# The down product in PSUM banks taken by name, in blocks of 512 columns, and six banks in turn for the products around the mixers

## The chip, the cores and the metric

The kernel runs on one core of one Trainium2 chip. The time is what the device takes from start to end of one launch, in microseconds; the value before is the median of three runs, 2753.59 us (2749.94, 2753.59, 2753.59). Beside them one execution was recorded by the hardware profiler; every duration below comes from that recording.

## The reference, cut to what matters

A decoder layer is computed for a prompt of 2048 tokens and for 8 sample sequences of 8 tokens (64 in all), with 1024 features. The part after the two mixers (a gated delta rule and a windowed attention) is:

```
x = x + g1 * (mix @ w_out)                          # out-projection, residual
h = rmsnorm(x) * (1 + sc2) + sh2
u = h @ ffn_w_up                                    # 1024 -> 2 x 2816
gate, up = split(causal_dwconv(u) + b)              # 3 taps
x = x + g2 * ((silu(gate) * up) @ ffn_w_down)       # 2816 -> 1024
y = rmsnorm(x, final_norm_w)
```

All values are float32.

## The kernel before

Features lie on the 128 partitions and tokens along the free axis, so a product is a weight tile of 128 x 128 that is loaded into TensorE and a block of tokens that streams past it. Every float32 operand is split into a high and a low part of a shorter type (a cast on ScalarE, L314 and L1600; the difference on VectorE, L315 and L1601), and each tile product is three matmuls: high by high, high by low, low by high. PSUM has eight banks of 512 float32 columns per partition, and a product accumulates in one bank until a vector engine reads it.

The stages follow each other: input projection and first mixers (to about 750 us), then `between(0)`, which does the out-projection of the first half (`outproj`, L1130 on, tile `op_ps`) and starts the up products (`up_proj`, L1209 on; the matmuls are those of `gemm_steps`, L323, tile `up_ps`). The other up groups of the first half fill TensorE beside the second set of mixers. `between(1)` does the same for the second half and starts the first six up groups of it. The rest of the second half's up products are done as `up_quarters`, by a Strassen scheme with few waits (L1503 and L323, tiles `uq_a`, `uq_u`, `uq_b`, `uq_g`, `uq_c`; ScalarE copies the last ones out in L1527). Each up result goes through a convolution (`conv`, L1427 on: taps on VectorE in a PSUM tile of three banks, `cq`, L1433) and the product of gate and up, `actq` (L1481), and lands in DRAM as `act_d`.

`outproj` and the ordinary up groups take their accumulator from two banks in turn (`acc_bank`, L394, and in `project`, L366, the tag "acc"): the matmul that starts a group waits until the group two earlier has been read. The readers are for `op_ps` the residual (VectorE, L1184; for the 64 sample columns L1187 and L1188) and for `up_ps` the taps (VectorE, L522) and copies with bias (ScalarE, L517).

`down_phase` (L1566 on) computes the last product with a Strassen-Winograd scheme: seven half-size products instead of eight. Its table `DOWN` names for each product the weight sum (A11, S2 and so on), the operand sum (B11, T2 and so on), the column group g, whether a fresh accumulator begins, and which output quarters the accumulator is added to. There are two passes of 512 columns each per half; in pass 2 the quarters of group 1 carry the 64 samples too, 576 columns. A product has KH = 11 k-steps; a k-step has four row tiles m, times two column blocks s (256 and 256, or 256 and 320), times three matmuls (L1690). So a product keeps eight accumulators, one in each bank.

Around the products: `get_w` and `get_t` load and split the operands, some k-steps ahead (DR = 6 ready, AHEAD = 3). Most operand sums were prepared in DRAM; T2 is made here from two loads and one VectorE subtraction (L1621), T4 from two loads and one addition (L1626). After the last k-steps of a product, taken bank by bank, `out` adds the accumulator to the output quarter (`residual`) and, from the fourth product on, adds its squares to a running sum (L1195, L1196). `norm` (L1646 on) turns these sums into a factor for each token by small matmuls (`ss_ps` in L214, `rb_ps` in L222, which also take a bank) and multiplies (L1654, L1660, L1662) and stores the output. It is a generator that is stepped between k-steps of the next product.

The eight banks came from a pool of their own, `psd`, with one tag and eight buffers, made after the quarters' pool was closed; which bank is which follows from the order of the requests. Where fewer than eight could be free (at the start, and where a norm was under way), the first LEAD = 5 k-steps ran on the first banks only ("head") and then on the others. These lines are in the part `if len(acc) < KT or not q` of `down_phase`.

The order of instructions on each engine is set by a scheduler from the program; each engine works through its own list in order, and a tile that is written again waits for its readers.

Of the kernel before, what the change touches and what calls it, by code (L numbers as in the profile page):

```python
# [14 lines left out]
F32 = mybir.dt.float32  # L15
# [7 lines left out]
P = 128  # L23
# [71 lines left out]
def kernel(  # L95
# [298 lines left out]
    def acc_bank(name):  # L394
        return pm.tile([P, 512], F32, tag="acc", name=name, bufs=BANKS["acc"])

# [732 lines left out]
    def outproj(hf, bis, mix, sums, op, kept=None):  # L1129
# [78 lines left out]

    def up_proj(hf, h, uc, op, ms=range(MU)):  # L1209
# [24 lines left out]
        return project(ms, "up_ps", lambda m: load_split(I["w_upT"][m]), h, hf, evac, turn=(3, 2), third=third)  # L1234
# [304 lines left out]
    def weight_sums(units, pool):  # L1539
# [3 lines left out]
        for i in units:  # L1543
# [22 lines left out]
    def down_phase(ds, dr, psd):  # L1566

        G, fw = MOD[:, 5], nw[:, 2]
        bk = lambda name: psd.tile([P, 512], F32, tag="dn", name=name)
# [61 lines left out]
        blocks_of = lambda q, g: [slice(0, SW), slice(SW, wide(q, g))]  # L1631
        queue = [(q, i, slice(0, wide(q, DOWN[q % ND][2]))) for q in range(Q - 1) for i in range(KH)]
        queue += [(Q - 1, i, blocks_of(Q - 1, 1)[s]) for s in (1, 0) for i in range(KH)]
# [12 lines left out]
        def norm(g, parts, x, sums, cols, last=False):  # L1646

            for off, n in parts:
# [6 lines left out]
                yield from token_rstd([a[:, off:off + n] for a in sums], n, rB, dr, bk)  # L1655
# [13 lines left out]
        for q in range(Q):  # L1669
# [6 lines left out]
            subs = blocks_of(q, g)  # L1676
            order = [(m, s) for m in range(NM) for s in range(2)]
            if new:
                banks = [bk("dn_ps") for _ in order] if not finish else [bk("dn_ps") for _ in order[:FREE]]

                acc = dict(zip(order, banks if q else banks[:1] + banks[4:] + banks[1:4]))
# [12 lines left out]
            def out(m, s):  # L1694
                for og, tg in outs:
# [3 lines left out]
                    residual(v, acc[m, s], n, min(n, SW), G[:, NM * og + m], v, dr)  # L1699
# [3 lines left out]
                    if first and s == 0:  # L1703
                        sums[tg] = [dr.tile([P, big], F32, tag=f"dsum{tg}", name=f"dsum{tg}", bufs=2)]
# [8 lines left out]
            lead = 0  # L1713
            if len(acc) < KT or not q:
                lead = LEAD
                head = order[:FREE if q else 5]
                for i in range(lead):
                    ahead(f + min(i + AHEAD, DR - 1))
                    products(i, head)
                    if finish and i in (1, 3):  # L1720
# [356 lines left out]
```

## Time and profile before

| | |
|---|---|
| median of three runs | 2753.59 us |
| profiled execution, its own time | 2747.36 us |
| its span | 2745.6 us |
| mean granted clock of TensorE | 0.985 |
| TensorE busy | 2638.5 us (96%) |
| VectorE, ScalarE, GpSimd busy | 69%, 47%, 29% |
| up quarters | 1815 to 2235 us |
| down | 2235 to 2745.6 us |

The profiled execution is 6.2 us faster than the median of the runs and lies 1.8 us outside its own span. PE is TensorE's matmul queue, PEld its weight loads, DVE VectorE, ACT ScalarE, POOL GpSimd, SP the queue that issues DMAs. A matmul's duration in the profile contains the filling of the array and overlaps with the next one: what a matmul costs is the distance between two starts.

### The profile page before, as it was taken

Reading aid. Unit: us, or ns where it says so; the run is one execution under the profiler, and the core shown is the slowest. Engines: PE = TensorE matmul, PEld = TensorE weight load, DVE = VectorE, ACT = ScalarE, POOL = GpSimd, SP = SyncE. Lnnn points to the kernel's source line nnn. Section 1 sums busy time; section 2 is a strip of 40 time slices with the busy share of each in tenths; the row PEclk is TensorE's granted clock in tenths of the full one; section 3 lists DMA queues with packets and bytes.
Section 4 is the critical chain, followed back from the end, with each engine's and each line's share of the span. In section 5 each row is a group of like instructions: output and inputs, shape, how many; then the busy total and the mean of one; then the engine's idle time right before and its main releaser. Section 6 shows DMA issues by size and latency. Waiting matters only on the chain.

```text
span 2745.6 us, 52204 instructions
## 1 busy us (share of the span) xinstructions
PE 2638.5 (96%) x19404; PEld 2472.7 (90%) x19404; DVE 1891.1 (69%) x3936; ACT 1300.8 (47%) x3394; POOL 807.1 (29%) x711
## 2 busy tenths in 40 slices
PE   7998999999999899999999999899999989999997
PEld 6898987788999898888888899899999989999997
DVE  7667479898403888888667654786777666677666
ACT  6444265554322654555444543554555544444443
POOL 2025143442313422222121204345655500022021
PEclk9999999999999999999999999999999999999998
DMA  7677443332345452332255335314555458567754
GB/s 281 232 267 242 117 139 104 91 100 77 129 114 192 130 146 78 99 92 74 85 177 177 133 122 183 113 66 162 166 174 193 158 184 282 184 222 266 237 179 155
DMA packets 319099, 433.99 MB, mean 158 GB/s; under 512 B 83155, under 2 KB 224436, under 8 KB 318580
## 3 DMA queue, kind: packets, MB, share of 16 engines
q1 hardware_dynamic: 318844, 430.66, 48.6%
q8 instruction: 152, 2.49, 0.4%
q14 instruction: 103, 0.84, 0.1%
HBM read 316.25 MB, written 115.33 MB: 157 GB/s over the span
## 4 chain that ended last, share of the span: by engine, by line
PE 64%; DVE 19%; DMA 8%; issue 4%; ACT 3%; POOL 2%; SPq 0%; DVEq 0%; ACTq 0%; POOLq 0%
PE up_ps L323 16%; PE in_ps L323 12%; PE dn_ps L1690 10%; PE op_ps L323 6%; PE uq_b L1503 4%; DVE ev L522 3%; PE uq_c L1503 2%; PE uq_g L1503 2%; PE uq_u L1503 1%; DVE ht L258 1%; PE pv_ps L954 1%; PE as_ps L917 1%; DMA tr<-T_d 1%; DVE gt L699 1%; DMA tx<-act_d 1%
## 5 line engine op out<-in xcount | busy, mean ns | idle before, releaser
L323 PE MATMUL up_ps<-hi,w_hi 128*128 128x384 f32 (+2 forms) x1152 | 378.1, 328 | 7.8 <-ACT cv L517 7.7
L323 PE MATMUL up_ps<-hi,w_lo 128*128 128x384 f32 (+2 forms) x1152 | 373.1, 324 | 3.7 <-DVE w_lo L315 3.7
L323 PE MATMUL up_ps<-lo,w_hi 128*128 128x384 f32 (+2 forms) x1152 | 370.5, 322 | 0.0
L323 PE MATMUL in_ps<-hi,w_hi 128*128 128x384 f32 (+2 forms) x1056 | 346.9, 333 | 5.1 <-DVE ev L572 1.8
L323 PE MATMUL in_ps<-lo,w_hi 128*128 128x384 f32 (+2 forms) x1056 | 349.2, 331 | 2.2 <-DVE lo L265 1.3
L323 PE MATMUL in_ps<-hi,w_lo 128*128 128x384 f32 (+2 forms) x1056 | 347.2, 329 | 1.2 <-POOL w_lo L315 1.2
L1690 PE MATMUL dn_ps<-th,wh 128*128 128x256 f32 (+1 forms) x1192 | 333.2, 289 | 13.7 <-DVE actq L1481 9.7
L1690 PE MATMUL dn_ps<-tl,wh 128*128 128x256 f32 (+1 forms) x1192 | 340.6, 289 | 2.8 <-DVE tl L1601 2.8
L1690 PE MATMUL dn_ps<-th,wl 128*128 128x256 f32 (+1 forms) x1192 | 338.7, 288 | 0.0
L323 PEld LDWEIGHTS up_ps<-hi,w_hi 128*128 128x128 f32 x1152 | 218.0, 189 | 28.3 <-issue 15.1
L1690 PEld LDWEIGHTS dn_ps<-th,wh 128*128 128x128 f32 x1192 | 225.8, 193 | 15.0 <-issue 9.9
L1690 PEld LDWEIGHTS dn_ps<-tl,wh 128*128 128x128 f32 x1192 | 229.6, 193 | 4.2 <-DVE tl L1601 4.1
L323 PEld LDWEIGHTS up_ps<-hi,w_lo 128*128 128x128 f32 x1152 | 217.8, 189 | 12.8 <-issue 7.0
L1690 PEld LDWEIGHTS dn_ps<-th,wl 128*128 128x128 f32 x1192 | 229.0, 193 | 0.0
L323 PEld LDWEIGHTS up_ps<-lo,w_hi 128*128 128x128 f32 x1152 | 218.0, 189 | 7.2 <-issue 6.2
L323 PEld LDWEIGHTS in_ps<-hi,w_hi 128*128 128x128 f32 x1056 | 200.3, 191 | 17.8 <-issue 9.7
L323 PEld LDWEIGHTS in_ps<-lo,w_hi 128*128 128x128 f32 x1056 | 202.0, 191 | 15.1 <-issue 9.5
L323 PEld LDWEIGHTS in_ps<-hi,w_lo 128*128 128x128 f32 x1056 | 201.9, 191 | 6.6 <-issue 4.4
L314 ACT CAST w_hi<-w_raw 128x1024 fp32r<-128x1024 f32 x124 | 129.7, 1047 | 117.4 <-PE op_ps L323 44.9
L315 DVE TENSOR_TENSOR w_lo<-w_raw,w_hi 128x1024 fp32r<-128x1024 f32 x95 | 118.1, 1243 | 93.2 <-ACT w_hi L314 91.7
L522 DVE SCALAR_TENSOR_TENSOR ev<-rb,cw,ev 128x384 f32<-128x384 f32 (+1 forms) x216 | 149.0, 696 | 38.0 <-ACT ev L515 35.9
L1601 DVE TENSOR_TENSOR wl<-wr,wh 128x512 fp32r<-128x512 f32 x149 | 107.4, 722 | 81.2 <-ACT wh L1600 79.2
(531 smaller groups left out, 6690.0 us busy)
## 6 DMA issues: line engine op xcount, KB each, us to landing
w_raw<-in_w_upT_dram SPq DMA_DIRECT2D x50, 512.0 KB
wada<-in_w_ada_dram SPq DMA_DIRECT2D x44, 512.0 KB
w_raw<-in_w_inT_dram SPq DMA_DIRECT2D x44, 512.0 KB
wr<-ws_d SPq DMA_DIRECT2D x88, 256.0 KB
proj<-ev SPq DMA_DIRECT2D x88, 192.0 KB
d<-act_d SPq DMA_DIRECT2D x33, 512.0 KB
wr<-in_w_downT_dram SPq DMA_DIRECT2D x66, 256.0 KB
tr<-T_d SPq DMA_DIRECT2D x66, 256.0 KB
```

The lines of the kernel that those rows point to most:

```text
L258: nc.vector.scalar_tensor_tensor(t, x, S[:, k, 0:1], rB[:, :np_], ALU.mult, ALU.mult)
L314: nc.scalar.copy(hi, raw)
L315: (eng or nc.vector).tensor_tensor(lo, raw, hi.bitcast(F32), ALU.subtract)
L323: nc.tensor.matmul(ps[:, :n], a[:, k, :], b[:, k, :n], start=first is not False and k == ks[0] and i == 0, stop=last is not False and k == ...
L522: nc.vector.scalar_tensor_tensor(out, src(j), w[:, j:j + 1], out, ALU.mult, ALU.add)
L699: nc.vector.tensor_tensor(tv, G[:np_, j, j + 1:].unsqueeze(2).broadcast_to(shape), T0[:, j, 0:j + 1].unsqueeze(1).broadcast_to(shape), ALU ...
L917: nc.tensor.matmul(banks[v][:, 256 * g + P * k0:256 * g + 256], qs[r, g0 + g], kw[r, P * k0:], start=True, stop=True, tile_position=(64 * ...
L954: nc.tensor.matmul(pv_ps[64 * v:64 * v + 64, :], (vprev[0], vt)[half][:, 64 * v:64 * v + 64], PT[v, half], start=half == k0, stop=half == 1)
L1503: nc.tensor.matmul(bk[t][:, :nb], u[:, k], v[:, k], start=new and k == 0 and y == 0, stop=k == KG - 1 and y == 2, skip_group_check=True)
L1601: nc.vector.tensor_tensor(l, raw, h.bitcast(F32), ALU.subtract)
L1690: nc.tensor.matmul(acc[m, s][:, :n], w[q, i][a][:, c], th[b][:, v], start=new and i == 0 and y == 0, stop=i == KH - 1 and y == 2, skip_gro ...
```

## The change

It has four parts.

- `down_phase` is handed the pool of the quarters, `pq`, and takes five of its banks by their names (a, u, b, g, c) and the three-bank tile `cq`, of which it uses each third as a bank. A list, `free`, rotates: a new set of accumulators takes the first entries, which then go to its end. The head-first k-steps are gone.
- A product that has no sample columns runs in one block of 512 columns, with four accumulators: all of pass 1, and in pass 2 the fourth and fifth product (S1 and S4, of group 2).
- In `DOWN` the product A22 with T4 is now the sixth and A12 with B21 the last. The norm that belongs to the end of pass 1 is stepped during the fourth product of pass 2 (it ran from its first), that of the fifth product of pass 2 during the last. The last product takes its blocks with the 320-column half first in the list of banks too.
- `free_bank` gives six banks in turn, two each of the tags "acc", "fr" and "at", to `op_ps`, and to `up_ps` in those groups that are begun in `between(0)` and from `between(1)` on.

```diff
+    FREE_TAGS = ("acc", "acc", "fr", "fr", "at", "at")
+    turns = [0]
+
+    def free_bank(name):
+        turns[0] += 1
+        return bank(name, FREE_TAGS[turns[0] % len(FREE_TAGS)])
...
-                ps = acc_bank("op_ps")
+                ps = free_bank("op_ps")
...
-        return project(ms, "up_ps", lambda m: load_split(I["w_upT"][m]), h, hf, evac, turn=(3, 2), third=third)
+        return project(ms, "up_ps", lambda m: load_split(I["w_upT"][m]), h, hf, evac, turn=(3, 2), third=third,
+                       tags=up_tags)
...
-            ("S1", "T1", 2, True, [(1, 2)]), ("S4", "B22", 2, False, [(0, 2)]), ("A12", "B21", 1, True, [(0, 1)]),
-            ("A22", "T4", 1, True, [(1, 1)])]
+            ("S1", "T1", 2, True, [(1, 2)]), ("S4", "B22", 2, False, [(0, 2)]), ("A22", "T4", 1, True, [(1, 1)]),
+            ("A12", "B21", 1, True, [(0, 1)])]
...
-        bk = lambda name: psd.tile([P, 512], F32, tag="dn", name=name)
+        free = [pq.tile([P, 512], F32, tag=t, name="dn_ps", bufs=1) for t in "aubgc"]
+
+        three = pq.tile([P, 3 * 512], F32, tag="cq", name="dn_ps", bufs=1)
+        free += [three[:, 512 * i:512 * i + 512] for i in range(3)]
...
-        blocks_of = lambda q, g: [slice(0, SW), slice(SW, wide(q, g))]
+        def blocks_of(q, g=None):
+
+            if q < ND or q % ND in (3, 4):
+                return [slice(0, PW)]
+            return [slice(0, SW), slice(SW, wide(q, g or DOWN[q % ND][2]))]
...
+            if last:
+                order = [(m, b) for b in (1, 0) for m in range(NM)]
             if new:
...
+                acc = dict(zip(order, free))
+                free = free[len(order):] + free[:len(order)]
...
-            if j == 4:
-                finish = norm(2, [(0, PW)], x, sums[2], cols[2])
+
+            if j == 4 and not ip:
+                finish = norm(2, [(0, PW)], x, sums[2], cols[2], free[4:6])
+            elif j == 4:
+                late = (2, [(0, PW)], x, sums[2], cols[2])
+            elif j == 5 and ip:
+                finish = norm(*late, free[-2:])
             elif j == 6:
-                finish = norm(1, [(0, PW)], x, sums[1], cols[1])
+                late = (1, [(0, PW)], x, sums[1], cols[1])
+            elif j == 2 and ip:
+                finish = norm(*late, free[-2:])
...
+            up_tags[:] = FREE_TAGS
             filler, _ = between(0, in_end(), es, range(MU))
+            up_tags[:] = ["acc"]
...
-        down_phase(ds, dr, new_pool(es, "psd", bufs=8, space=PSUM))
+        down_phase(ds, dr, pq)
```

Counted over the program, TensorE has 1188 matmuls fewer, VectorE 49 instructions fewer, ScalarE 24, GpSimd 21 and the DMA queue 11.

How the order of TensorE reads where the quarters end and down begins. Before (dn_ps_24944, 24948 and so on are single banks of the pool; behind a row, in brackets, the engines whose work it waits for):

```order
L323 MATMUL uq_b_24882<-hi2_19793,rl_21099 128x320
L1690 MATMUL dn_ps_24944<-th_24960,wh_24954 128x256 [waits Activation_49]
L1690 MATMUL dn_ps_24944<-tl_24961,wh_24954 128x256 [waits DVE_49]
L1690 MATMUL dn_ps_24944<-th_24960,wl_24955 128x256
L1690 MATMUL dn_ps_24948<-th_24960,wh_24954 128x256 [waits DVE_49,PE_49,Activation_49]
L1690 MATMUL dn_ps_24948<-tl_24961,wh_24954 128x256
L1690 MATMUL dn_ps_24948<-th_24960,wl_24955 128x256
L1690 MATMUL dn_ps_24949<-th_24960,wh_24954 128x256
```

Changed (dn_ps_24940 is bank a, 24941 u, 24942 b, 24943 g):

```order
L323 MATMUL uq_b_24882<-hi2_19793,rl_21099 128x320
L1713 MATMUL dn_ps_24940<-th_24954,wh_24948 128x512 [waits Activation_49]
L1713 MATMUL dn_ps_24940<-tl_24955,wh_24948 128x512 [waits DVE_49]
L1713 MATMUL dn_ps_24940<-th_24954,wl_24949 128x512
L1713 MATMUL dn_ps_24941<-th_24954,wh_24948 128x512 [waits Activation_49]
L1713 MATMUL dn_ps_24941<-tl_24955,wh_24948 128x512
L1713 MATMUL dn_ps_24941<-th_24954,wl_24949 128x512
L1713 MATMUL dn_ps_24943<-th_24954,wh_24948 128x512
```

The blocks are twice as wide, and the second bank waits for ScalarE where it waited for VectorE, TensorE and ScalarE.

TensorE where S1 of pass 1 ends and S4 adds to the same banks, in the changed kernel (dn_ps_24944 is bank c, dn_ps_24945 the tile of three banks; the first row and its two predecessors write the second third, the next nine the third one, and the last row begins S4 in the first third):

```order
L1713 MATMUL dn_ps_24945<-th_26007,wl_26002 128x512
L1713 MATMUL dn_ps_24945<-th_25959,wh_25953 128x512 [waits DVE_49]
L1713 MATMUL dn_ps_24945<-tl_25960,wh_25953 128x512
L1713 MATMUL dn_ps_24945<-th_25959,wl_25954 128x512
L1713 MATMUL dn_ps_24945<-th_25983,wh_25977 128x512
L1713 MATMUL dn_ps_24945<-tl_25984,wh_25977 128x512
L1713 MATMUL dn_ps_24945<-th_25983,wl_25978 128x512
L1713 MATMUL dn_ps_24945<-th_26007,wh_26001 128x512
L1713 MATMUL dn_ps_24945<-tl_26008,wh_26001 128x512
L1713 MATMUL dn_ps_24945<-th_26007,wl_26002 128x512
L1713 MATMUL dn_ps_24944<-th_26118,wh_26112 128x512 [waits Activation_49]
L1713 MATMUL dn_ps_24945<-th_26031,wh_26025 128x512 [waits DVE_49]
```

Before, the same passage goes from one bank to the next (each a tile of its own; the wait of each is for VectorE's read of that bank):

```order
L1690 MATMUL dn_ps_26253<-th_26133,wl_26128 128x256
L1690 MATMUL dn_ps_26254<-th_26133,wh_26127 128x256 [waits DVE_49]
L1690 MATMUL dn_ps_26254<-tl_26134,wh_26127 128x256
L1690 MATMUL dn_ps_26254<-th_26133,wl_26128 128x256
L1690 MATMUL dn_ps_26249<-th_26145,wh_26139 128x256 [waits Activation_49]
L1690 MATMUL dn_ps_26249<-tl_26146,wh_26139 128x256
L1690 MATMUL dn_ps_26255<-th_26133,wh_26127 128x256 [waits DVE_49]
```

In the changed kernel the wait before the nine matmuls of the last third is for VectorE's read of the second third, and that of the last row for its read of the last third.

VectorE near its end, before (x11 are rows of the output, drB the factor of each token, dsum1 the sum of squares; the five products with drB are the norm of the 320-column half):

```order
L1662 SCALAR_TENSOR_TENSOR x01_28238<-x01_28238,nw_84,drB_31098 128x320 [waits Activation_49]
L1662 SCALAR_TENSOR_TENSOR x01_28238<-x01_28238,nw_84,drB_31098 128x320 x3
L1662 SCALAR_TENSOR_TENSOR x11_28962<-x11_28962,nw_84,drB_31098 128x320
L1184 SCALAR_TENSOR_TENSOR x11_28962<-dn_ps_30754,MOD_83,x11_28962 128x256 [waits PE_49]
L1184 SCALAR_TENSOR_TENSOR x11_28962<-dn_ps_30756,MOD_83,x11_28962 128x256 [waits PE_49]
L1184 SCALAR_TENSOR_TENSOR x11_28962<-dn_ps_30758,MOD_83,x11_28962 128x256 [waits PE_49]
```

Changed:

```order
L1192 SCALAR_TENSOR_TENSOR x01_27029<-dn_ps_24940,MOD_83,x01_27029 128x256 [waits PE_49]
L1192 SCALAR_TENSOR_TENSOR x01_27029<-dn_ps_24941,MOD_83,x01_27029 128x256 [waits PE_49]
L1204 TENSOR_TENSOR dsum1_29304<-dsum1_29304,sq_29873 128x256 [waits Activation_49]
L1204 TENSOR_TENSOR dsum1_29304<-dsum1_29304,sq_29886 128x256 [waits Activation_49]
L1192 SCALAR_TENSOR_TENSOR x01_27029<-dn_ps_24942,MOD_83,x01_27029 128x256 [waits PE_49]
L1683 SCALAR_TENSOR_TENSOR x01_27029<-x01_27029,nw_84,drB_29721 128x320 [waits Activation_49]
L1683 SCALAR_TENSOR_TENSOR x01_27029<-x01_27029,nw_84,drB_29721 128x320 x3
L1683 SCALAR_TENSOR_TENSOR x11_27897<-x11_27897,nw_84,drB_29721 128x320
L1192 SCALAR_TENSOR_TENSOR x01_27029<-dn_ps_24943,MOD_83,x01_27029 128x256 [waits PE_49]
```

The five products of the norm stood ahead of all four last residuals and now stand ahead of the last one alone.

More of the change, by code (lines that the diff above doesn't have):

```diff
@@ L1207, in up_consts @@
         return d
+    up_tags = []
     def up_proj(hf, h, uc, op, ms=range(MU)):
@@ L1654, in norm @@
                     nc.scalar.mul(xs[m], xs[m], fw[:, m:m + 1])
-                yield from token_rstd([a[:, off:off + n] for a in sums], n, rB, dr, bk)
+                yield from token_rstd([a[:, off:off + n] for a in sums], n, rB, dr, lambda name: next(two))
                 if last:
@@ L1712, in down_phase @@
             f = place[q, 0, 0] if not last else place[q, 0, SW]
[L1713 to L1720, printed above, removed]
-                        next(finish)
-                if q:
-                    acc.update({c: bk("dn_ps") for c in order[FREE:]})
-                for i in range(lead):
-                    products(i, order[len(head):])
+            ahead(f + AHEAD)
             with tc.issue_after(fetched[0]):
```

39 lines of the change are left out of this document (20 added, 19 removed).

## Prediction

> **What bounds the kernel now.** I read the page first, then busy time by stage, then the list of waits of PE in each stage, then the timeline where a wait was long. The page says that TensorE carries the span:
>
> ```profile
> span 2745.6 us, 52204 instructions
> PE 2638.5 (96%) x19404; PEld 2472.7 (90%) x19404; DVE 1891.1 (69%) x3936; ACT 1300.8 (47%) x3394; POOL 807.1 (29%) x711
> ```
>
> By stage (columns: window, length, busy time of PE, PEld, DVE, ACT, POOL, then granted clock, DMA share, GB/s) the rows are: out-projection between the mixers, the same for the second half with the first ordinary up groups, the up quarters, down.
>
> ```profile
> 735.00:922.00 187.00, 179.08 (x1093) 177.89 (x1092) 63.62 (x83) 64.38 (x119) 62.26 (x51) 0.97 0.53 167
> 1626.00:1815.00 189.00, 176.48 (x1044) 173.98 (x1043) 121.35 (x198) 88.00 (x188) 65.67 (x57) 0.97 0.42 139
> 1815.00:2235.00 420.00, 417.58 (x2523) 415.54 (x2522) 299.91 (x353) 225.71 (x463) 221.82 (x216) 1.00 0.50 166
> 2235.00:2745.60 510.60, 477.98 (x3774) 473.34 (x3774) 335.20 (x583) 218.93 (x412) 69.82 (x72) 0.97 0.65 215
> ```
>
> The quarters are a solid block of PE (2.4 us idle in 420). Down idles 33 us in 511, at a clock of 0.97. So the time is the number of matmuls times their spacing, plus few holes, and the change touches both. A hole closed in front of the quarters is kept, because PE has work all the way to down.
>
> **The start of down (term B).** The timeline of PE where the quarters end (start, duration, engine, line, operation, idle before and its releaser), and the clock after it:
>
> ```profile
> 2234.39 0.31 PE L323 MATMUL uq_b<-hi,rl 128*128 128x320 f32 x1
> 2235.94 0.39 PE L1690 MATMUL dn_ps<-th,wh 128*128 128x256 f32 x1 [1.24 <-ACT rbu L1527]
> ...
> 2236.28 0.28 PE L1690 MATMUL dn_ps<-th,wl 128*128 128x256 f32 x1
> 2246.25 0.55 PE L1690 MATMUL dn_ps<-th,wh 128*128 128x256 f32 x1 [9.69 <-DVE actq L1481]
> 2240.00:2250.00 10.00, 3.75 (x17) 3.78 (x18) 5.67 (x6) 1.51 (x3) 0.00 (x0) 0.50 0.43 156
> 2250.00:2260.00 10.00, 10.00 (x78) 10.00 (x77) 0.62 (x2) 1.27 (x3) 0.00 (x0) 0.89 0.31 104
> ```
>
> Down's banks come from a pool of its own, laid over the quarters' banks. The first waits for the copy of the quarters' last result (1.24 us); the next four wait until DVE has read the three-bank tile for the last time, in the activation product of L1481 (9.69 us). Then the clock is 0.50 to 2250 and 0.89 over the next ten. At 0.50 the loss is half the time: half of the 3.75 us to 2250, and with 11% of ten microseconds missing another 1.1, so 3.0; I take 2.7, since the first matmul after the wait is partly the wait itself. Changed: the first product writes banks a, u, b, g by name, each of which waits only for its own copy, and the three-bank tile isn't touched before the fourth product. The DVE work that ended the wait still runs, beside PE; the operand splits of k-step 7 and on are queued between its pieces, and six k-steps lie ready in front of them (16 us at the spacing below). So B = −(1.2 + 9.7 + 2.7) = −13.6, call it −14; bounds −11 (PE waits once more for a split, or part of the slow clock stays) and −14.
>
> The Trainium skill ("TensorE: Matmul & The Clock Gate", part 1 on the clock gate) states that the array falls to half clock after an idle window of about 3.4 us and comes back after as long a busy one. Here the trace agrees on the 9.69 us hole; a row further down does not.
>
> **Merging to 512 columns (term A).** The order of the changed kernel holds 1188 matmuls fewer: all of pass 1 and the products S1 and S4 of pass 2 write 512 columns at once where they wrote 256 twice. What a matmul costs is the spacing of starts; an even stretch in down at 256 columns, one in the quarters at 384, and the only pairs at 512 columns on a full array (a pair as one row, then durations min/median/max):
>
> ```profile
> 2329.12 0.28 PE L1690 MATMUL dn_ps<-th,wl 128*128 128x256 f32 x1
> ...
> 2331.40 0.28 PE L1690 MATMUL dn_ps<-th,wh 128*128 128x256 f32 x1
> 1815.78 0.34 PE L1503 MATMUL uq_b<-hi,rh 128*128 128x384 f32 x1
> ...
> 1817.19 0.34 PE L1503 MATMUL uq_b<-hi,rl 128*128 128x384 f32 x1
> 265.49 0.62 PE L653 MATMUL d_ps<-gm,tgtr 128*128 128x512 f32 x2
> L653 PE MATMUL d_ps<-gm,tgtr x34: 276/394/502, 265.5 to 1428.6; 128*128 128x512 f32 x32, 64*64 64x256 f32 x2
> ```
>
> Nineteen steps in 2.28 us are 120 ns at 256 columns; eight in 1.41 are 176 at 384. The line through both (0.44 ns a column) gives 232 at 512; the pair gives 620 − 394 = 226. I take 230: a merged pair saves 2 × 120 − 230 = 10 ns, and A = 1188 × 0.010 = −12 us. Bounds: 226 gives −17, 234 gives −7. It is small because the array's time goes by columns: only the fixed part, some 10 to 14 ns a matmul, is saved once per pair.
>
> **Six banks in turn (terms C, D).** The waits of PE in the first and the second of the two out-projections with the up groups behind them (total, times, longest):
>
> ```profile
> PE up_ps L323 <- ACT cv L517: 2.2, 1, 2.2
> PE up_ps L323 <- ACT cv L517: 5.5, 1, 5.5
> PE op_ps L323 <- DVE sres L1187: 2.5, 1, 2.5
> ```
>
> Each is a matmul that waits for one of two accumulators to be read. With six in turn the reader may be four groups late. C = −2.2 (bounds −2.4 and 0). In the second place, 5.5 + 2.5 = 8 us are bank waits; but the engines that evacuate are then late by as much, and the next group can wait for its split weights instead, so I take half, D = −4 (bounds −1 and −7). DVE and ACT are busy 121 and 88 of 189 us there, so the rest can be worked off later.
>
> **A new wait (term E).** Three of the eight banks are slices of one tile. In the order, a matmul that goes on in one third waits for the DVE read of another third, since the tile is followed as a whole: 17 such waits, of which 5 have under 0.7 us of other matmuls between the producing matmul and the wait, 7 have 2 to 2.8 us, the rest more. Priced by the nearest wait for a residual and what stands in DVE's queue:
>
> ```profile
> PE dn_ps L1690 <- DVE x L1184: 1.2, 1, 1.2
> L1184 DVE SCALAR_TENSOR_TENSOR x<-dn_ps,MOD,x 128x256 f32<-128x256 f32 x128 | 57.7, 479 | 14.0 <-PE dn_ps L1690 13.7
> L1601 DVE TENSOR_TENSOR wl<-wr,wh 128x512 fp32r<-128x512 f32 x143 | 103.3, 724 | 79.8 <-ACT wh L1600 77.8 <-PE dn_ps L1690 1.7
> ```
>
> Five at 1.2 us less what covers them is +5. Bounds: +3 (some covered), +9 (the seven at the edge are caught behind a 0.72 us split, +0.6 each). Behind the waiting matmul stands all of PE.
>
> **The end (term F).** The clock and waits of the last product, and what DVE does ahead of its last residuals:
>
> ```profile
> 2716.00:2722.00 6.00, 6.00 (x32) 6.00 (x32) 2.87 (x8) 1.66 (x4) 0.82 (x1) 0.53 0.32 92
> 2730.00:2745.60 15.60, 2.50 (x12) 2.17 (x12) 6.84 (x15) 3.10 (x8) 3.14 (x4) 0.61 0.37 130
> PE ss_ps L214 <- DVE dsum L1196: 4.7, 2, 3.2
> PE dn_ps L1690 <- DVE tl L1601: 3.8, 7, 1.0
> 2725.61 4.36 DVE L1662 SCALAR_TENSOR_TENSOR x<-x,nw,drB 128x320 f32<-128x320 f32 x5 [2.86 <-ACT drB L223]
> ```
>
> With B21 last, DVE no longer adds two loads for each k-step there, so the 3.8 us of waits for splits mostly go, and of the slow clock (0.47 of 6 us, 2.8) perhaps half: −5. Against it, the order puts the statistics of the 320-column half later against PE: 15 matmuls follow its broadcast where 38 did, 23 × 0.12 = 2.8 us nearer to the end, and the 4.36 us of norm stand ahead of the last residual. F = −5 + 3 = −2 (bounds −6 and +3).
>
> By the same page of the skill the half clock of the row at 2716 should not be there, with no hole over 3.2 us before it: the measurement decides.
>
> **What T4 now shares (term G).** T4 in sixth place runs beside a norm. Rows of DVE and of two busy windows (DMA share and GB/s last):
>
> ```profile
> L1626 DVE TENSOR_TENSOR tr<-tr,tx 128x512 f32<-128x512 f32 x11 | 8.6, 783 | 3.0 <-DMA tx<-E_d 2.1 <-DMA tr<-T_d 0.8
> L1662 DVE SCALAR_TENSOR_TENSOR x<-x,nw,drB 128x512 f32<-128x512 f32 x12 | 21.0, 1808 | 10.9 <-ACT drB L223 10.9
> 2270.00:2280.00 10.00, 10.00 (x85) 10.00 (x85) 6.25 (x12) 2.52 (x5) 0.00 (x0) 1.00 0.98 325
> 2300.00:2310.00 10.00, 10.00 (x85) 10.00 (x85) 6.85 (x13) 4.15 (x7) 0.00 (x0) 1.00 0.87 289
> ```
>
> A k-step there takes PE 12 × 0.230 = 2.76 us and DVE 0.78 + 0.72 + 0.72 = 2.2; eleven are 30.4 and 24.5, and four norm steps of 1.8 add 7.2. DVE is level with PE, with six k-steps of stock: G = 0 (bounds 0 and +4).
>
> **Sum.** −14 − 12 − 2 − 4 + 5 − 2 = −29 us against the profiled run of 2747.4: 2718. The median of the runs shown is 6.2 above the profiled one, so 2724.
>
> **Rivals.**
> 1. Operands, not PE, set the pace at 512 columns. For it: DMA at 0.98 and 325 GB/s in a row above, DVE level with PE beside T4. Against: PE is busy 10.00 of 10 in those same windows, and a k-step gets only 4% shorter. Then A is lost and G costs 4: 2724 + 12 + 4 = 2740. Chance 0.16.
> 2. The fixed part vanishes at 512, since the next weights load wholly under the longer stream. At 0.42 ns a column (56 ns more for 128 columns is 0.44) that is 216 ns: 24 ns a pair, A = −28.5, time 2708. Against: the fixed part doesn't shrink from 256 to 384 columns. Chance 0.08. The Trainium skill (same page, "Back-to-back issue gap") gives columns/2.4 + 2.5 ns, 216 at 512; by it 256 columns would take 109, and the trace has 120.
> 3. Slower: the cross-third waits are each followed by a slow clock, as the row at 2716 is by waits of a few microseconds. At 0.53 for 6 us one costs 1.2 + 2.8 = 4.0. All other terms are −34, so from 9 such waits of the 17 on the change loses; with 12, +14: 2768. Against: the 1.24 us wait at 2235 alone and the 1.2 us one for a residual have no row of slow clock. Chance 0.05.
> 4. The start isn't freed: the quarters' tail keeps DVE, and down's first splits arrive no earlier than now. Then B is lost: 2738. Against: the splits of the first six k-steps stand in the order of DVE ahead of the last taps. Chance 0.09.
>
> The forecast has 0.62. The range 2708 to 2742 reaches from rival 2 over 4 to rival 1; it leaves out rival 3 and the worst of rival 1. About 0.2% (5.5 us) is what a measurement of this kernel can tell from no change; faster 0.90, same 0.05 (rival 1 with the worst of E), slower 0.05.
>
> **What would show it.** In the changed profile: the first dn_ps matmul within 0.5 us of the last uq_b, no wait for actq, clock 1.00 at 2240; starts 0.23 apart at 512 columns (0.216: rival 2); waits of PE for x of 1 to 1.5 us, some five, in the products S4 and T2 to B22 of pass 2; no wait of up_ps for cv before 1815. Wrong would be waits of PE for tl or th of more than 5 us in T2 or T4 (rival 1), or a clock under 0.9 in the middle of down (rival 3).

## The result, and the profile after

The changed kernel takes 2723.54 us (median of four runs, 2722.54 to 2724.44), the one before 2753.0 on the same chip: the ratio is 0.9895 with a 95% interval of 0.9878 to 0.9912, 29.5 us less. The forecast was 2724, 29 less. The two profiled executions differ by less, 2747.36 against 2722.96 us, since the profiled one of before was a quick one and the one of after reached its first `op_ps` matmul 4.5 us later (823.3 against 818.7), in code that the change doesn't touch. From that matmul on they differ by 28.9 us. The total is thus met, but the parts below aren't all what the forecast made them.

The page of the changed kernel, its span and busy times:

```profile
span 2721.2 us, 49667 instructions
PE 2626.3 (97%) x18216; PEld 2411.2 (89%) x18216; DVE 1890.1 (69%) x3885; ACT 1295.2 (48%) x3370; POOL 805.5 (30%) x690
```

Its busy times by stage, for the second out-projection with the first up groups, the quarters, and down (columns as in the prediction):

```profile
1626.00:1810.00 184.00, 177.97 (x1072) 176.37 (x1071) 123.63 (x201) 88.95 (x197) 66.95 (x57) 0.99 0.44 144
1810.00:2230.00 420.00, 416.61 (x2514) 413.88 (x2514) 300.30 (x353) 223.34 (x460) 222.74 (x216) 1.00 0.49 166
2230.00:2721.00 491.00, 460.56 (x2586) 406.72 (x2584) 331.98 (x532) 215.11 (x388) 65.99 (x51) 0.98 0.68 223
```

Down is 20 us shorter, and it begins 4.9 us earlier although the run was 4.5 us late at its first `op_ps` matmul. But PE still idles 30 us in down: the holes moved. Where the quarters end, the timeline of PE now has no gap at all, and the clock stays full (the windows behind it):

```profile
2229.48 0.31 PE L323 MATMUL uq_b<-hi,rl 128*128 128x320 f32 x1
2229.62 0.40 PE L1713 MATMUL dn_ps<-th,wh 128*128 128x512 f32 x1
...
2230.00:2240.00 10.00, 10.00 (x46) 8.24 (x45) 7.16 (x10) 6.59 (x12) 0.20 (x1) 1.00 0.60 216
2240.00:2250.00 10.00, 10.00 (x46) 8.29 (x45) 9.77 (x16) 5.12 (x9) 0.00 (x0) 1.00 0.89 298
2250.00:2260.00 10.00, 9.75 (x44) 7.73 (x42) 5.94 (x10) 3.00 (x6) 0.00 (x0) 1.00 0.99 350
2260.00:2270.00 10.00, 7.17 (x25) 5.80 (x26) 6.65 (x11) 1.57 (x3) 0.00 (x0) 0.83 1.04 380
```

In the last of these windows the work stops. The timeline of PE there, at the change from the first product to the second:

```profile
2258.91 0.39 PE L1713 MATMUL dn_ps<-th,wh 128*128 128x512 f32 x1
2259.14 0.39 PE L1713 MATMUL dn_ps<-tl,wh 128*128 128x512 f32 x1
2259.36 0.39 PE L1713 MATMUL dn_ps<-th,wl 128*128 128x512 f32 x1
2262.83 0.48 PE L1713 MATMUL dn_ps<-th,wh 128*128 128x512 f32 x1 [3.08 <-DVE x L1192]
...
2263.96 0.63 PE L1713 MATMUL dn_ps<-th,wh 128*128 128x512 f32 x1
2264.39 0.63 PE L1713 MATMUL dn_ps<-tl,wh 128*128 128x512 f32 x1
```

Two things are to be read here. Starts at full clock are 0.227 us apart at 512 columns (the median over down as well). And a hole of 3.08 us for a residual, with starts 0.43 apart behind it: half clock (0.83 over these ten microseconds). The four longest rows of PE's waits in down say what the holes are now (total, times, longest):

```profile
PE dn_ps L1713 <- DVE x L1192: 11.0, 9, 3.1
PE dn_ps L222 <- DVE dg L218: 5.1, 2, 3.7
PE dn_ps L214 <- DVE dsum L1204: 3.9, 1, 3.9
PE dn_ps L1713 <- DVE tl L1616: 0.6, 1, 0.6
```

The 9.7 us for actq are gone and the waits for splits too (3.8 before), but residuals cost 11.0 where they cost 1.2, and 3.7 us of a wait for dg (the diagonal tiles that a norm's small matmuls read) in the middle of down are new.

### The profile page after: what moved, and what is told of

Read it like the earlier page. It is cut to its first block, busy times and chain, and to the rows that moved or that the text cites. A ratio compares the mean times of both kernels' runs of the same rounds, so it can differ in the third digit from the quotient of the medians.

```text
span 2721.2 us, 49667 instructions
## 1 busy us (share of the span) xinstructions
PE 2626.3 (97%) x18216; PEld 2411.2 (89%) x18216; DVE 1890.1 (69%) x3885; ACT 1295.2 (48%) x3370; POOL 805.5 (30%) x690
## 4 chain that ended last, share of the span: by engine, by line
PE 68%; DVE 15%; DMA 8%; issue 4%; POOL 3%; ACT 2%; SPq 0%; DVEq 0%; ACTq 0%; POOLq 0%
PE up_ps L323 20%; PE in_ps L323 13%; PE dn_ps L1713 10%; PE op_ps L323 6%; PE uq_b L1514 2%; DVE ev L530 2%; DMA tr<-T_d 2%; DMA rawu<-in_w_upT_dram 2%; PE as_ps L925 2%; PE pv_ps L962 1%; DMA rawg<-in_w_upT_dram 1%; PE uq_c L1514 1%; PE uq_u L1514 1%; PE uq_g L1514 1%; PE am_ps L680 1%
## 5 line engine op out<-in xcount | busy, mean ns | idle before, releaser
L1713 PE MATMUL dn_ps<-th,wh 128*128 128x512 f32 (+2 forms) x796 | 269.6, 345 | 12.0 <-DVE x L1192 11.0
L1713 PE MATMUL dn_ps<-tl,wh 128*128 128x512 f32 (+2 forms) x796 | 271.9, 343 | 0.7 <-DVE tl L1616 0.6
L1713 PE MATMUL dn_ps<-th,wl 128*128 128x512 f32 (+2 forms) x796 | 271.0, 343 | 0.0
L1713 PEld LDWEIGHTS dn_ps<-th,wh 128*128 128x128 f32 x796 | 149.9, 190 | 32.5 <-DVE x L1192 11.2
L1713 PEld LDWEIGHTS dn_ps<-tl,wh 128*128 128x128 f32 x796 | 151.0, 190 | 16.7 <-DVE tl L1616 1.1
L1713 PEld LDWEIGHTS dn_ps<-th,wl 128*128 128x128 f32 x796 | 150.8, 190 | 15.7
L1615 ACT CAST wh<-wr 128x512 fp32r<-128x512 f32 x149 | 92.2, 619 | 134.3 <-PE dn_ps L1713 76.8
```

The source lines that it names most:

```text
L1615: nc.scalar.copy(h, raw)
L1713: nc.tensor.matmul(acc[m, s][:, :n], w[q, i][a][:, c], th[b][:, v], start=new and i == 0 and y == 0, stop=i == KH - 1 and y == 2, skip_gro ...
```

## The experiments

Three groups, each with runs of the kernel before on its own chip (2753.2, 2754.5 and 2755.8 us), so kernels of different groups are compared by ratios and not by times; inside a group the medians can be compared too. "Down" is the time from the last matmul of the quarters to the end of the span in the profiled execution.

| kernel | us | ratio to before (95%) | down, us |
|---|---|---|---|
| before | 2753 | 1 | 511.2 |
| changed | 2721.3 | 0.9890 (0.9872 to 0.9908) | 490.4 (first profile 491.7) |
| eight tiles | 2713.5 | 0.9856 (0.9839 to 0.9874) | 480.7 |
| 512 columns split | 2726.6 | 0.9900 (0.9882 to 0.9919) | 497.3 |
| two banks in turn | 2737.8 | 0.9948 (0.9932 to 0.9965) | 495.6 |
| eight tiles, cq first | 2717.4 | 0.9862 (0.9849 to 0.9876) | 487.8 |
| eight tiles, stores from GpSimd | 2711.9 | 0.9840 (0.9825 to 0.9855) | 479.4 |
| eight tiles, T4 last | 2717.3 | 0.9863 (0.9849 to 0.9876) | 488.0 |
| eight tiles, dg by GpSimd | 2716.0 | 0.9858 (0.9842 to 0.9873) | 484.6 |
| banks dealt anew | 2718.5 | 0.9865 (0.9844 to 0.9885) | 487.2 |
| x later | 2725.1 | 0.9887 (0.9865 to 0.9908) | 493.6 |
| T2 plain | 2719.6 | 0.9869 (0.9847 to 0.9892) | 491.7 |
| banks anew and x later | 2718.4 | 0.9863 (0.9841 to 0.9885) | 489.9 |

My theory was the forecast's: the start, the merging and the banks bring what was reckoned, and the tile of three banks takes some back. The main rival was that VectorE or the loads set the pace of down, so that holes only move.

**The base.**

> The changed kernel once more, as the base of the others in this group: 2723.5 us within 2.

It came to 2721.3, with holes in the same places in its profile; their sizes differ a little. Waits for residuals are 9.2 us here (3.7 of them in the hole at the second product) where the first profile has 11.0 (3.1), so an effect of 2 us can't be read from one pair of profiles.

**Tiles of their own for the three banks.**

```diff
-        free = [pq.tile([P, 512], F32, tag=t, name="dn_ps", bufs=1) for t in "aubgc"]
-        three = pq.tile([P, 3 * 512], F32, tag="cq", name="dn_ps", bufs=1)
-        free += [three[:, 512 * i:512 * i + 512] for i in range(3)]
+        eight = [pq.tile([P, 512], F32, tag=f"dn{t}", name="dn_ps", bufs=1) for t in "buagcxyz"]
+        free = [eight[i] for i in (2, 1, 0, 3, 4, 5, 6, 7)]
...
-        down_phase(ds, dr, pq)
+        down_phase(ds, dr, new_pool(es, "psd", space=PSUM))
```

> The changed kernel with eight tiles of one bank each in place of five banks and the tile of three. Theory: nine holes of PE in front of dn_ps matmuls behind 2300 us of the changed profile (1.00, 0.64, 1.83, 0.66, 0.54, 0.95, 1.42, 0.97 and 1.83 us, 9.8 in all) are there because a third of the tile waits for the read of another third; with tiles of their own each matmul has at least 3.4 us of other matmuls in front of its wait, so 8 to 10 us go: 2714 to 2716 us. The hole of 3.1 us at 2263 is a wait of bank a and stays. Rival: VectorE reads the banks late anyway, behind the splits in its queue, and the holes only move: 2721 to 2724 us, the sum of the waits for x as before.

It takes 7.9 us less by the medians, as the theory said, and 10 to 11 less in down. PE's longest waits in its down:

```profile
PE dn_ps L1711 <- ACT th L1613: 5.0, 1, 5.0
PE dn_ps L1711 <- DVE tl L1614: 3.2, 2, 2.1
PE dn_ps L222 <- DVE dg L218: 2.4, 2, 1.4
PE dn_ps L1711 <- DVE x L1192: 2.4, 2, 1.7
PE dn_ps L214 <- POOL dsum L1204: 1.3, 1, 1.3
```

Without the hole at the second product, residuals cost 2.4 us in place of 7.9 (5.5 in the base run). So 3 to 5.5 us of those waits weren't for the bank that a matmul writes, but for a neighbour in the same tile. New are 7.1 us for operands, 2.1 for the last k-step of the first product (tl) and 5.0 in the second (th): their loads stand in SP's queue behind the store of the quarters' last result, which waits for VectorE; in the changed kernel the same loads had come in front of that store. So the expectation was wrong in one point: the hole at the second product didn't stay 3.1, it grew.

The waits across the thirds aren't the whole gain. From the last matmul of the last product to the end it is 12.8 us here and 16.3 in both profiles of the changed kernel, so 3.5 of the ten stand there. The order of VectorE isn't the same at this place. Here the norm of the 320-column half stands ahead of all four last residuals, in the changed kernel ahead of the last one alone. VectorE with eight tiles, and then in the changed kernel:

```profile
2693.45 4.36 DVE L1681 SCALAR_TENSOR_TENSOR x<-x,nw,drB 128x320 f32<-128x320 f32 x5 [2.01 <-ACT drB L223]
2697.73 0.86 DVE L1192 SCALAR_TENSOR_TENSOR x<-dn_ps,MOD,x 128x256 f32<-128x256 f32 x2
```

```profile
2704.16 0.48 DVE L1192 SCALAR_TENSOR_TENSOR x<-dn_ps,MOD,x 128x256 f32<-128x256 f32 x1
2704.56 3.79 DVE L1683 SCALAR_TENSOR_TENSOR x<-x,nw,drB 128x320 f32<-128x320 f32 x5
2708.28 0.47 DVE L1192 SCALAR_TENSOR_TENSOR x<-dn_ps,MOD,x 128x256 f32<-128x256 f32 x1
```

In the changed kernel the last statistics come behind the 3.79 us of norm, and PE waits 3.9 us for dsum there, where it waits 0.9 here. So this run changes two things, the tiles and the order at the end; what the second brings is close to the 3 us that term F had charged for it.

**The 512 columns in two halves.**

```diff
-                        nc.tensor.matmul(acc[m, s][:, :n], w[q, i][a][:, c], th[b][:, v],
+                        for u0, u1 in [(0, SW), (SW, PW)] if n == PW else [(0, n)]:
+                            nc.tensor.matmul(acc[m, s][:, u0:u1], w[q, i][a][:, c],
+                                             th[b][:, v.start + u0:v.start + u1],
...
```

> The changed kernel with each 512-column matmul of down written as two of 256 into the same bank; banks, waits and loads as they were. By the starts in the changed profile (0.227 at 512, 0.120 at 256) 1188 x (0.240 - 0.227) = 15 us more: 2739 us. By the forecast's 0.230 it is 12: 2735.5. If the operands set the pace in down (rival 1) the time stays within 4 us of the changed kernel. If the fixed part vanished at 512 (rival 2) it would be 28: 2752.

The accumulation of a bank is begun twice in it, once for each half, so that the sums of these products are not the reference's. The medians give 5.3 us more (the intervals overlap), the profile 6 to 7 in down, where 15 were expected. The time without holes did grow by some 15 us: a product of 512-column matmuls without a hole takes 29.9 us in the changed kernel and 31.7 here, and down has nine such products. But from the last matmul of the quarters to the last product matmul it is 479.8 us here and 475.4 and 474.2 in the two profiles of the changed kernel, so holes and slow clock fell by 9 to 11. Three of its waits, beside those of the changed kernel above:

```profile
PE dn_ps L1714 <- DVE x L1192: 3.4, 4, 1.8
PE dn_ps L1714 <- DVE sres L1195: 1.9, 1, 1.9
PE dn_ps L1714 <- ACT wh L1615: 1.2, 1, 1.2
```

So the merging saves its 15 us of TensorE, and some 10 of them are lost in holes. Most of that is waits for residuals (3.4 here, 9.2 and 11.0 there): with a shorter product they come late. That is neither rival 1 (nothing saved) nor the plain sum. How much of the 15 is left is known from the profiles to 1 or 2 us; the runs alone, with their overlapping intervals, don't show it.

**Two banks in turn.**

```diff
-                ps = free_bank("op_ps")
+                ps = acc_bank("op_ps")
...
-            up_tags[:] = FREE_TAGS
+            up_tags[:] = ["acc"]
...
```

> The changed kernel with the two banks acc in turn for op_ps and up_ps again, down as changed. By the forecast's terms C and D 6 us more: 2729.5. By the holes of the two traces in these places (17.1 against 14.4, 21.8 against 13.1) 11 more: 2734.5. Rival: what is won there is given back where the quarters wait for their inputs, so 0 to 3 more.

It takes 16 us more (2737.8 against 2721.3), more than either. Between the last `op_ps` matmul and the last `up_ps` matmul lie 83.7 us; in the two profiles of the changed kernel it is 72.9 and 73.7, before 83.4. PE's waits in its second out-projection and up groups, the same as before:

```profile
PE up_ps L323 <- ACT cv L525: 5.5, 1, 5.5
PE op_ps L323 <- DVE sres L1195: 2.5, 1, 2.5
```

Neither row is in that list for the changed kernel. So 10 us are gained in this one stretch. From first to last matmul the quarters take 419.5 us here, as before (419.1), and 419.8 to 424.3 in the runs with six banks: 1 to 5 are given back, the rival's mechanism at a smaller size. One wait at their start is in both profiles of the changed kernel and neither here nor before:

```profile
PE uq_b L1514 <- DVE rl L1375: 1.7, 1, 1.7
```

The rest lies in two other places. From the first `op_ps` matmul to the first one of the second half it is 810.8 us here and 804.8 and 803.4 in the changed kernel, where the wait of 2.2 us for cv is gone that is back here; and down is 4 to 5 us longer (495.6). Before has 807.1 in the first of these places, so that not all of its 6 to 7 us belong to the banks; what the others are I didn't separate.

**The wait at the start, undone alone.**

```diff
-        free = [eight[i] for i in (2, 1, 0, 3, 4, 5, 6, 7)]
+        free = [eight[i] for i in (5, 6, 7, 2, 1, 0, 3, 4)]
```

> The kernel with eight tiles, with the three banks under the tile cq as the first three of down, so that its first matmul waits for the last read of cq again (term B undone alone). By term B of the forecast 14 us more: 2727.5. Rival: a part of what the start gains is given back 30 us later, where PE waits 7.1 us for operands in the kernel with eight tiles; with PE late at the start these are there in time, and the net is 5 to 7 us: 2718.5 to 2720.5.

The wait is back, and it is the only one of PE in the first 60 us of down:

```profile
PE dn_ps L1711 <- DVE actq L1492: 11.1, 1, 11.1
```

Down is 7.1 us longer than with eight tiles; by the ratios it is 1.7 (intervals overlap). Only 4.0 of the 7.1 lie where the start acts: from the last matmul of the quarters to the last of the second product it is 73.7 us here and 69.7 with eight tiles. Another 2.8 are in the sixth product, where two profiles of the changed kernel differ by 5.5 among themselves. So the rival's mechanism is right, and the size is below its 5 to 7: of a start that comes 11 us earlier some 4 stay in this kernel, since the first two products then wait for operands that the wait at the start had given time for. In the changed kernel itself, whose hole at the second product is smaller, the start was not undone.

**The store out of the way.**

```diff
-            nc.sync.dma_start(act_d[p, :, c0:], act)
+            (nc.gpsimd if p == MI - 1 else nc.sync).dma_start(act_d[p, :, c0:], act)
...
-            nc.sync.dma_start(ts_d["E"][i], d12)
+            (nc.gpsimd if p == MI - 1 else nc.sync).dma_start(ts_d["E"][i], d12)
```

> The kernel with eight tiles, with the last two stores of the up quarters (actq and E) issued from GpSimd's queue in place of SP's; the orders of TensorE, VectorE and ScalarE are the same. Theory: in the kernel with eight tiles PE waits 7.1 us for split operands in the second product, because SP's queue stands 7.2 us in front of that store (it waits for VectorE) with down's loads behind it; without it the waits shrink to 1 or 2 us and the time by 5 to 7: 2707 to 2709 us. Rival: the loads are late for lack of DMA bandwidth (share 0.98 in 2245 to 2255), so nothing or 1 us: 2712 to 2714.

The ratio is the lowest of all, 0.9840, but the interval overlaps that of eight tiles, and the hole is little smaller. SP's longest wait from 2236 to 2262, in the kernel with eight tiles and then here (total, times, longest; 8.8 is the longest):

```profile
SPq L1493 <- DVE actq L1492: 7.2, 1, 7.2
```

```profile
SPq L1607 <- DVE wl L1614: 11.1, 5, 8.8
```

The same time is now spent by the next load, which waits for its buffer until VectorE has made a split; and that split stands behind the quarters' last convolution in VectorE's own order. PE's wait for th is 4.8 us where it was 5.0 (with that for tl 5.3 in all, where it was 7.1). The theory named the right queue, but the store was only the first of two things that stood there. The rival, too little DMA bandwidth, isn't excluded for the rest.

**T4 last again.**

```diff
-            ("S1", "T1", 2, True, [(1, 2)]), ("S4", "B22", 2, False, [(0, 2)]), ("A22", "T4", 1, True, [(1, 1)]),
-            ("A12", "B21", 1, True, [(0, 1)])]
+            ("S1", "T1", 2, True, [(1, 2)]), ("S4", "B22", 2, False, [(0, 2)]), ("A12", "B21", 1, True, [(0, 1)]),
+            ("A22", "T4", 1, True, [(1, 1)])]
```

> The kernel with eight tiles, with A22 and T4 last and A12 and B21 sixth, as before. By term F (waits of the last product for splits 3.8 us and half of a slow clock, 5 us saved by the move) less 0 for G: 5 us more, of which the end of the norm may take back 3: 2715.5 to 2718.5. Rival: beside a norm T4 costs as much as it does at the end (VectorE level with PE there, waits for dg and dsum), so no change or faster: 2710 to 2714.

By the ratios 2 us more, within the noise; down is 7.3 us longer in the profile. From 2600 on its PE waits are

```profile
PE dn_ps L1711 <- DVE tl L1614: 4.2, 1, 4.2
PE dn_ps L222 <- DVE dg L218: 2.1, 2, 1.4
PE dn_ps L214 <- DVE dsum L1204: 2.1, 1, 2.1
```

against tl 1.1, dg 1.4, dsum 0.9 (and 2.4 for residuals) with eight tiles. The wait for the sum of two loads is there again in the last product, 3.1 us of it: this part of term F holds. The last product takes 46.6 us where it took 40.3. But the sixth product, which T4 has left, is shorter, 31.7 for 36.3 in pass 1 and 35.3 for 38.2 in pass 2: beside a norm T4 does cost something. Whether the order is worth 2 or 7 in all stays open.

**dg by GpSimd.**

```diff
-            nc.vector.tensor_scalar_mul(dg[:, j], ident, r[:, j:j + 1])
+            (dg_on or nc.vector).tensor_scalar_mul(dg[:, j], ident, r[:, j:j + 1])
```

> The kernel with eight tiles, with the diagonal tiles dg of the norms within down made by GpSimd, which has rtok anyway, in place of VectorE. Theory: in the changed kernel PE waits 3.7 us for dg at 2420, because dg stands in VectorE's queue behind a split that waits for a late load; in the kernel with eight tiles this wait is 1.0 us, so 1 us less: 2712.5, and the waits of rb_ps matmuls before 2690 go to zero. Rival: no change, or slower by what GpSimd takes for dg (over 1 us for four tiles) where PE reaches the matmul first: 2713.5 to 2716.

The very last norm keeps VectorE here. No gain (0.9858 against 0.9856). The wait for the dg that moved got longer, from 1.0 us to 4.2:

```profile
PE dn_ps L222 <- POOL dg L218: 4.2, 2, 3.7
```

GpSimd takes 4.48 us for the four tiles of a dg (2408.19 on) where VectorE takes 0.87, so it is not a better place for it; the rival had it right. What the wait in the changed kernel comes from is seen in VectorE's timeline there:

```profile
2415.09 0.15 DVE L142 TENSOR_SCALAR rsq<-dn_ps 128x4 f32<-128x4 f32 x1
2418.96 0.69 DVE L1616 TENSOR_TENSOR tl<-tr,th 128x512 fp32r<-128x512 f32 x1 [3.71 <-ACT th L1615]
2419.57 0.87 DVE L218 TENSOR_SCALAR dg<-cst,rtok 128x128 f32<-128x128 f32 x4
```

VectorE stands 3.71 us in front of a split whose input is late, with dg ready to run behind it, and PE with its matmuls of rb behind that.

**Banks dealt anew, x later, T2 plain.** These, and the last run, start from the changed kernel itself. In the first, a set of four banks holds thirds of the tile only at every second place:

```diff
+                if q == 3:
+                    c, t0, t1, t2, a, u, b, g_ = free
+                    free = [c, t0, a, t1, u, t2, b, g_]
                 acc = dict(zip(order, free))
```

> The changed kernel (tile of three banks kept) with the banks of the fourth product dealt out anew: c, first third, a, second third, then u, last third, b, g, so that thirds no longer follow each other. By the theory of waits across the thirds nearly every such wait has 3 us or more of other matmuls in front of it (five under 0.7 us before, none now; three of 1.2 to 1.8 remain), and the start of down stays as in the changed kernel, without the operand wait of the kernel with eight tiles: 8 us less than the changed kernel, 2713.5, or a little below the kernel with eight tiles. Rival: the waits come from VectorE's queue and stay: 2720 to 2723.

By the ratios 0.9865 against 0.9890 for the changed kernel, some 7 us (intervals overlap), 3 to 5 in the profiles. It still waits 8.6 us for residuals, 4.1 of them in the one hole at the second product, and 4.3 for splits; without that hole residuals are 4.5, where the two profiles of the changed kernel have 7.9 and 5.5. The direction is the theory's, with a size between it and the rival; taken alone it isn't clear of the noise.

The other two were to show what fills the hole at the second product. In one the load of x for that product (1 MB) is issued later:

```diff
+            if j != 1 or ip:
+                x_load()
...
+                if i == 3:
+                    x_load()
```

> The changed kernel with the 1 MB load of x for the second product issued three k-steps later. If the hole of 3.1 us at 2263 (VectorE behind an addition that waits for T2's loads) comes from DMA bandwidth (share 0.99 and 1.04, 350 to 380 GB/s there), these loads land up to 3 us earlier and the hole shrinks to under 1: 2718 to 2720. Rival: the loads wait for their buffers and not for bandwidth: no change, 2721 to 2723.5.

The hole is 4.0 us, no smaller, and the time is that of the changed kernel (0.9887). In the other the second load of T2 and the subtraction are left out, so that its sums are not the reference's:

```diff
-                raw, more = get("tr", "T1", r, RAWS), get("tx", "B22", slice(r.start, min(r.stop, PW)), 2)
-                c = more.shape[1]
-                nc.vector.tensor_tensor(raw[:, :c], more, raw[:, :c], ALU.subtract)
+                raw, c = get("tr", "T1", r, RAWS), PW
```

> The changed kernel with T2 left out in part: T1 alone is used, without the second load (B22, 256 KB a k-step) and the subtraction. If these set the pace of the second product the hole at 2263 goes with the slow clock behind it (3.1 + 1.6 us) and pass 2 loses its few waits for splits: 5 us less than the changed kernel, 2716 to 2718. Rival 1 of the forecast in full (operands set the pace throughout) would give over 10 less; if neither matters, 2721 to 2723.5.

The time is 0.9869, 6 us under the changed kernel by the ratios (intervals overlap), but down is as long as in it, and the hole is 2.8 us. VectorE's waits in 2240 to 2264 of that run:

```profile
DVE wl L1616 <- ACT wh L1615: 7.2, 3, 5.5
DVE x L1192 <- DMA x<-x2T: 1.5, 1, 1.5
```

Without T2's addition the residual waits for its own x, whose load (issued at 2249.5, with that of the second product) lands 8 us later. So the hole has more than one cause: take one away, and another ends it. That x was asked for too late, behind loads of the second product in SP's queue, is likely; issuing it earlier was not tried.

> Both of the above, banks dealt out anew and x later: the gains add, 2710 to 2712; if only the banks matter, as the run with the banks alone.

The combination is as the banks alone (0.9863), so the later load adds nothing.

## Why the prediction was right, term by term

| term | forecast (bounds) | measured |
|---|---|---|
| B, start of down | −14 (−11 to −14) | no wait and clock 1.00: −14 at the place; 3.1 us and 1.7 of slow clock come back 30 us later. The first two products take 77.4 us before, 64.8 and 66.3 after; less 3.6 for merging −7.5 to −9 |
| A, merging | −12 (−7 to −17) | spacing 0.227, 1188 x 0.013 = −15 of TensorE; undone alone +5 in the medians (intervals overlap), +6 to +7 in down |
| C, first out-projection | −2.2 (0 to −2.4) | the wait of 2.2 is gone |
| D, second out-projection | −4 (−1 to −7) | −10 between the last op_ps and the last up_ps, +1 to +5 in the quarters |
| E, waits across the thirds | +5 (+3 to +9) | waits for residuals 1.2 to 11.0, without the hole of 3.1 +7 (+4 in the second profile); with eight tiles 3 to 5.5 of that go |
| F, the end | −2 (−6 to +3) | waits for splits 3.8 to 0.6, for dsum 4.7 to 3.9, last matmul to end 16.2 and 16.3: about −4 |
| G, T4 beside a norm | 0 (0 to +4) | +3.7 for dg, and 1.7 lost to a slow clock behind it |

The likeliest case came true in kind. The start of down, the merging and the bank waits are in the profile where the forecast put them, and so are some of the new waits of the tile of three; 3.7 of the 7.9 us lie in the sixth product of pass 2, which the forecast doesn't name, and 2.4 stay there with eight tiles, so that these are waits for the bank itself. Three sizes were off, and they made up for each other. That the sum came out within a microsecond is luck.

- Term D was mis-sized: half of the 8 us was taken off for evacuating engines that fall behind. They hardly held PE up: the whole 8 went, and 2 more. Only the 1 to 5 us that the quarters take longer are of the kind that I feared.
- Term B was right at its place, but the step "six k-steps lie ready in front of them" looked only at operands. The first product ends 30 us in, and there residual and operands of the second are late, because the pause in front had given loads and VectorE's queue their time. With the pause back in the kernel with eight tiles, PE has no other wait there; the start is worth some 4 us in it, not 14.
- Term A was reckoned as if the matmuls were alone. A pair takes 5% less time when merged, so there is less time to read a bank, and about half of the saving reappears as waits for residuals (9.2 and 11.0 us, against 3.4 with the columns split). The forecast kept A and E as independent terms, and they are not.

Rival 1 (operands set the pace) was wrong as a whole, since windows of down stand at 10.00 busy of 10 at the new spacing, but right in two places, 2260 and 2420. Rival 2 (216 ns at 512 columns) is out: 0.227. The Trainium skill ("TensorE: Matmul & The Clock Gate", "Back-to-back issue gap") gives 216 for a matmul by itself and about 131 for a stream of weight loads and matmuls, which this is; neither is what was measured here. Rival 3 (each cross-third wait with a slow clock behind it) didn't happen as a rule. Its sign, a clock under 0.9 in the middle of down, is there twice (0.83 from 2260 and from 2415), but behind the hole at the second product and the wait for dg, which are no cross-third waits. The waits of up to 1.8 us left the clock alone in this profile:

```profile
2385.00:2395.00 10.00, 8.33 (x37) 6.55 (x37) 5.66 (x8) 3.34 (x6) 2.59 (x2) 1.00 0.49 150
```

The idle 1.67 of this window is one wait (1.8 us from start to start), and the clock is 1.00. But the second profile of the same kernel has one place where waits for residuals did bring a slow clock: behind one of 1.2 us (at 2622.6) and one of 0.8 (at 2624.8), 256-column matmuls start 0.21 apart where 0.120 is full speed.

```profile
2624.00:2628.00 4.00, 3.04 (x12) 2.79 (x12) 4.00 (x5) 3.77 (x7) 3.84 (x3) 0.57 0.46 151
```

So the mechanism exists and cost 1.7 us (0.43 of 4) once in two profiles; it is the sixth product of pass 2, so whether these waits are cross-third ones isn't shown. Rival 4 (the start not freed) is refuted by the first matmul 0.14 us behind the quarters.

## What to carry to other kernels

Follow every wait to the tile and not to the bank: slices of one tile are waited for as a whole, and a list of "who waits for whom" with the matmul time between the two ends shows before anything runs where waits can come. When a stall in front of a stage goes, look at the first change of buffers behind it, where the loads that had been filling up in the pause are asked for at once. And don't add the saving of shorter work to the price of new waits as if they were independent: the shorter work makes part of the waits. When a run is to undo one thing alone, compare the orders of the other engines too: with eight tiles a norm had moved as well.

## What the runs showed of the hardware

A hole of 3.1 us in PE is followed by starts 0.43 us apart where 0.227 is full speed (2262.83 on), one of 1.7 us at 2389.8 is not. The length of the hole alone doesn't decide it. In other profiles half clock follows holes of 1.2 us (the base run, 0.57 from 2624 to 2628), 1.3 us (eight tiles, 0.83 from 2400 to 2410) and 1.9 us (512 columns split, 0.83 from 2490 to 2500), while the clock stays at 1.00 behind one of 2.7 us (the base run, 2410 to 2420) and one of 2.8 us (T2 plain, 2258 to 2268). A clock of 0.83 over ten microseconds, or 0.57 over four, is half clock for 3.4 us. The Trainium skill ("TensorE: Matmul & The Clock Gate", part 1) has half clock set in after an idle window of about 3.4 us, and lets that window run freely. The 3.4 us agree with the lengths seen here, but a hole of 1.2 us is no such window, and so the measurement and that sentence differ.

At full speed the starts are 0.120 us apart at 256 columns, 0.147 at 320, 0.175 at 384 and 0.227 at 512. These lie on a line of 0.42 ns a column and a fixed part of some 13 ns, so the fixed part doesn't go away with longer streams. And the loads reached 350 to 380 GB/s in the windows of 2250 to 2270, above the 325 of the prediction's row and the 338 of the fastest ten microseconds that I saw in down before (2520 to 2530).
